# Low parts of weights by a negated copy and an accumulating transfer instead of a VectorE subtraction

## The chip, the cores and the metric

The kernel runs on one core of a Trainium2 chip. The metric is the device time of one execution in microseconds (us). The core has five engines with queues of their own, each worked through in order: TensorE (PE in the profile), VectorE (DVE), ScalarE (ACT), GpSimd (POOL) and SyncE (SP), which here issues the loads of weights. GpSimd and SyncE issue transfers (DMA) that 16 DMA engines carry out.

## The reference

One layer of a diffusion backbone over 128 context tokens and 512 latent tokens of width 1024, all in float32:

```python
def trunk_layer(x, cond, C0, n0, m0, rows, w_mod, ...):
    mod = jax.nn.silu(cond) @ w_mod + b_mod
    sh1, sc1, g1, shm, scm, gm, sh2, sc2, g2 = jnp.split(mod, N_MOD, axis=-1)
    h = modulate(rmsnorm(x, norm_g[0]), sh1, sc1)
    x = x + 0.5 * g1[:, None, :] * swiglu(h, ffn1_w1, ffn1_w2)
    h = modulate(rmsnorm(x, norm_g[1]), shm, scm)
    y, C, n, m = mixer(h, C0, n0, m0, rows, w_in, b_in, ...)
    x = x + gm[:, None, :] * y
    h = modulate(rmsnorm(x, norm_g[2]), sh2, sc2)
    x = x + 0.5 * g2[:, None, :] * swiglu(h, ffn2_w1, ffn2_w2)
    return x, C, n, m

def swiglu(h, w1, w2):
    a, b = jnp.split(h @ w1, 2, axis=-1)
    return (jax.nn.silu(a) * b) @ w2
```

The mixer projects h by w_in (9232 columns) to queries, keys, values, gates and the inputs of a short convolution, scans four heads in both directions in chunks of 128 tokens (mLSTM), and leads the results through w_ml_out, w_sc_out and w_o. At the end there is one more norm.

## The kernel before

**Products in three parts.** TensorE multiplies in a reduced form of float32 (float32r). So that nothing is lost, each operand is split in a high part, the rounded value, and a low part, the rest. A product is three matmuls of 128 x 128 weights against 320 tokens: high weights with high activations (line 238), high weights with low activations (239), low weights with high activations (240). The 640 tokens stand transposed, in two halves of 320.

**Splitting.** `split` makes both parts: ScalarE copies the raw values into a float32r tile (line 73), then VectorE subtracts that from the raw values (line 74). Weights use the tiles `wr` (raw, 128 x 1024, five buffers), `wh` and `wl` (high and low, 128 x 512, six buffers each). Activations use tiles named H..h and H..l, Uh and Ul, Bh and Bl, and go through the same function.

**Pairs.** Most of the projections (72 pairs of 128-column blocks) use Winograd's form of Strassen's algorithm: seven products in the place of eight, in the order A11, S1, S2, A12, S3, S4, A22. A11, A12 and A22 are blocks of the raw weights themselves, the "own blocks"; S1 to S4 are sums and differences of blocks that VectorE (for some pairs GpSimd) writes into `ws` tiles (line 211). Each product has 12 matmuls. Between the products ScalarE or VectorE copies partial sums out of PSUM or from one bank to another (lines 266, 272, 276, 284, 287, 290).

**Plain column blocks.** The second matrices of the feed-forwards (w2), w_ml_out, w_sc_out and most of w_o are multiplied block by block by `plain_el`: one raw tile, one or two operands of up to 512 columns, both token halves. `head_el` (the three pairs behind a norm) and `halves_el` (the last column blocks ahead of a norm) split their operands too. So do some units of the modulation, whose other units work from the raw tiles in float32 or on VectorE and are strewn between the elements.

**The order.** All is written out in one program, and each engine does its share in that order. `op()` hands out the next operand and first has the operands up to four places ahead cast (`cast_more`). A raw tile counts as done when its last reader has been emitted, and `load_more` then issues the next load on SyncE's queue, which waits until the buffer's readers are through:

```python
            split(o["ap"], hi[:, :w], lo[:, :w])
            optile[n] = (hi, lo)
            ptr["cast"] += 1
            rdone.update(o["last"])
            load_more()
```

**GpSimd** issues the transfers that hold no weights: x to and from memory between the mixer and the rest (`spill_x`, line 1058; line 1577), gates' rows and their products (1178, 1225, 1424), head results, the cached states (1248), new states (1330). It also adds a few tiles (lines 211, 752, 1229) and clears the two raw tiles of the gate columns (`gate_load`, line 1049), whose loads are the first of the mixer's head.

Of the kernel before, what the change touches and what calls it, by code (L numbers as in the profile page):

```python
# [44 lines left out]
def mixer_step(ctx: ExitStack, tc: tile.TileContext, x_prompt, x_sample, state_C, state_n, state_m,  # L45
# [26 lines left out]
    def split(raw, hi, lo):  # L72
        A.copy(hi, raw)  # L73
        V.tensor_sub(lo, raw, f32(hi))  # L74

    # ------------------------------------------------------------ program: weights run ahead of their use
    RAWB, OPB, SB, AHEAD = 5, 6, 4, 4
    raws, ops = [], []
    rtile, optile, rdone = {}, {}, set()
# [17 lines left out]
    def cast_more(upto):  # L97
        load_more()
        while ptr["cast"] < min(upto, ptr["held"] + OPB, ptr["cap"], len(ops)):
            n = ptr["cast"]  # L100
            if not ready(ops[n]):
                return
            while ptr["sum"] < min(n + 2, len(ops)) and ready(ops[ptr["sum"]]):
                o = ops[ptr["sum"]]
                o["ap"] = o["src"](o)
                ptr["sum"] += 1
            o = ops[n]
            w = o["n"]
            hi = ring.tile([P, 512], F32R, name="wh", bufs=OPB)
            lo = ring.tile([P, 512], F32R, name="wl", bufs=OPB)  # L110
            split(o["ap"], hi[:, :w], lo[:, :w])
            optile[n] = (hi, lo)
            ptr["cast"] += 1
            rdone.update(o["last"])
            load_more()
# [56 lines left out]
    def element(raws_, ops_, emit):  # L172
        return {"raws": raws_, "ops": ops_, "emit": emit}

    def step(fn):
        return element([], [], fn)
# [19 lines left out]
                              dap(w, row0 * ncol + col0, [[ncol, P], [P * ncol, nk], [1, P]]))  # L196
        return load

    # ------------------------------------------------------------ products
    # One pair of 128-column blocks of weights against both token halves: seven products (Winograd's form  # L200
    # of Strassen's algorithm over column blocks, halves of the contraction and halves of the tokens).
    LH, RH = slice(0, 512), slice(512, 1024)

    def pair_ops(r1=0, r2=1, e1=None):
        e1 = e1 or V

        def total(key, engine, fn, a, b):
            def src(o):
                g = o["group"].setdefault(r1, {})
                t = g[key] = ring.tile([P, 512], F32, name="ws", bufs=SB)  # L210
                getattr(engine, fn)(t, part(o, a), part(o, b))  # L211
                return t
            return src

        def part(o, key):
            if key[0] == "S":
                return o["group"][r1][key]
            return rtile[o["base"] + (r1 if key[1] == "1" else r2)][:, LH if key[2] == "1" else RH]

        whole = lambda key: lambda o: part(o, key)  # L220
        spec = lambda src, *r: {"raws": list(r), "n": 512, "src": src}
        return {
            "A11": spec(whole("A11"), r1), "A12": spec(whole("A12"), r1), "A22": spec(whole("A22"), r2),
            "S1": spec(total("S1", e1, "tensor_add", "A21", "A22"), r2),
            "S2": spec(total("S2", V, "tensor_sub", "S1", "A11"), r1, r2),
            "S3": spec(total("S3", e1, "tensor_sub", "A11", "A21"), r1, r2),
            "S4": spec(total("S4", V, "tensor_sub", "A12", "S2"), r1, r2),
        }
# [17 lines left out]
            late.pop(0)()  # L246

    def relax(left=1):
        """Emit what can wait no longer, with this many calls to come."""
        while lazy and len(lazy) >= left:  # L250
            lazy.pop(0)()

# [43 lines left out]
            yield  # L296

    def pair_el(load1, load2, ev, e1=None, units=(), spare_v=False):
        """units: elements with operands of their own, put between the products."""
        po = pair_ops(e1=e1)  # L300
        at_ = {1 + 2 * i: u for i, u in enumerate(units)}
        loads, ops_ = [load1, load2], []
        for i, name in enumerate(ORDER):
            ops_.append(po[name])
            if i in at_:
                ops_ += [dict(o, raws=[len(loads)], src=(lambda t, c: lambda o: rtile[o["base"] + t][:, c:c + 512])(
                    len(loads), c)) for c, o in zip((0, 512), at_[i]["ops"])]
                loads += at_[i]["raws"]

        def emit():  # L310
            nf = len(fill)
            for i, _ in enumerate(pair_steps(ORDER, ev, spare_v)):
                if i in at_:
                    at_[i]["emit"]()
                relax(7 - i)
                drain(nf - nf * (i + 1) // 7)
        return dict(element(loads, ops_, emit), pair=True)
# [20 lines left out]
        return HB["12" if k < 4 else "22"][k % 4]  # L338

    def head_el(p, chain, work, mid=()):  # L340
        """The three pairs behind a norm, without Strassen: three left halves first, row block by row block as the
        norm yields them, then what mid holds, while the right halves are made."""
        pre = len(mid) // 2
        order = [None] * pre + [0, 1, 2] + [None] * (len(mid) - pre) + [3, 4, 5]
        at_ = {t: i for i, t in enumerate(order) if t is not None}
# [56 lines left out]
        return el  # L402

    def halves_el(loads, nk, acts, ev, after):
        """Column blocks whose left halves all come first, then their right halves."""
        per = (nk + 3) // 4

        def emit():
# [34 lines left out]
    def plain_el(load, nk, acts, ev, halves=(0, 1)):  # L443
        def emit():
            nf = len(fill)
            ps = {h: big() for h in halves}
            w = [op() for _ in range(0, nk, 4)]
            n = 0
            for k in range(nk):
                hi, lo = w[k // 4]  # L450
                for h in halves:
                    three(ps[h][:, :HT], hi, lo, k % 4, acts(k, h), k == 0, k == nk - 1)
                relax(nk - k)
                drain(nf - nf * (k + 1) // nk)
            for h in halves:
                ev(h, ps[h][:, :HT])
            squares()
        return dict(element([load], tile_ops(nk), emit), calm=True)

    # ------------------------------------------------------------ constants  # L460
    zero = tp.tile([P, HT], mybir.dt.bfloat16, name="nrow")
    G.memset(zero, 0.0)
    ones = cst.tile([P, P], F32, name="ones")
# [39 lines left out]
            G.dma_start(gb[32 * d:32 * d + 4, i:i + 1], dap(b_in, off + 4 * d, [[1, 4], [1, 1]]))  # L503
        G.dma_start(m0[32 * d:32 * d + 4, :], dap(state_m, 4 * d, [[1, 4], [1, 1]]))

    # Sums seeded by a copy into PSUM go on accumulating: every bank they use has been written by the PE once.
    for i in range(4):
        PE.matmul(big()[:, :HT], zero[:, :P], zero, start=True, stop=True)

# [26 lines left out]
    def col(name, i):  # L536
        return vT[:, rows[name] + i:rows[name] + i + 1]

    # ------------------------------------------------------------ modulation
    PO = {}  # L540

    def mod_load(ch, half, kq):
# [4 lines left out]
        return load  # L547

    def mod_cols(ch, m0_, n, p, parts):
        """Rows of the modulation to columns, in three steps."""  # L550
        w = 2 * parts
        S = {}

# [59 lines left out]
    after = []  # L613

    def mod_mix(ch, half):
        """Half of a channel: units with split operands and units in float32 by turns."""
        S = {}

        def emit(w, kq):
# [67 lines left out]
        return units  # L687

    def with_units(main, units, spare=0):
        """Spread modulation units over elements; what a unit leaves to be done follows an element later."""  # L690
        out = []
        n, m = len(main) - spare, len(units)
        e = 0
# [31 lines left out]
            V.tensor_scalar(modT[:, ch], modT[:, ch], 0.5, None, op0=OP.mult)  # L725
        return f

    # ------------------------------------------------------------ norms
    X = [None] * KT
    sq, SQ = {}, []  # L730
    PIECES = ((0, 128, 192), (320, 448, 512))
# [82 lines left out]
        return f  # L814

    def right_chain(n, sh, first=False):
        """Steps in the order of head_el, and the sums of Strassen's algorithm that it makes by the way."""
        def all_of(*fs):
            def f():
                for x in fs:  # L820
# [57 lines left out]
        while SQ:  # L878
            SQ.pop(0)()

    # ------------------------------------------------------------ feed-forward
    GROUPS = (6, 6, 6, 4)

    def ffn(w1, w2, g, norm_, lists, units, e1=None, mid=()):
        """Elements: [head], then per group the other pairs and the column blocks of w2."""
        head, els, f0 = [], [], 0
        for size in GROUPS:
            U = {}
# [44 lines left out]
                        f()  # L933
        return after

    # ------------------------------------------------------------ start: x, first norm
    PO["u_x"] = ExitStack()

    def open_u():
# [77 lines left out]
                   mod_dve(SH2, (0,), ma_wide), 2)  # L1017
    prog += [step(gain(1, SCM)), step(lambda: PO["ma_x"].close()), w2s[-1]]

    # ------------------------------------------------------------ mixer  # L1020
    xd = dr.tile([KT, P, T], F32, name="xd")
    rd = dr.tile([KT, P, T], F32, name="rd")
    td = dr.tile([KT, P, T], F32, name="td")
# [214 lines left out]
    def head_steps(h):  # L1238
# [101 lines left out]
            return f  # L1340

        def rs_begin():
            """The mean squares to the power -0.5, by Newton's iteration from an estimate on the bits."""
            x = S["ss"]
            w = S["rs"] = PO["mlp"].tile([P, 2, NCH], F32, name="hrs")
            I32 = mybir.dt.int32
# [82 lines left out]
    def cx_pair(m):  # L1429
        def ev(mi, h, src):  # L1430
# [25 lines left out]
            for o, i in segs:  # L1456
                lazy.extend([side(o, i, True, False, w0), side(o, i, False, True, w2)])
        return z_load(C_OFF + m * P), z_load(X_OFF + m * P), ev

    h0 = head_q(0)  # L1460
    chain, work = right_chain(1, SHM)
    prog.append(head_el([(gate_load(IG_OFF), gate_load(FG_OFF), gate_ev), h0[0], h0[1]], chain, work,
                        mod_pe(GM, (0,), False)))
    prog += [step(spill_x), step(close_u), step(open_h1)]
    gate, NG = gates(), 38
    h1 = head_q(1)
    prog += weave([pair_el(*j, spare_v=True) for j in (h0[2], gml_pair(0), h1[0], h1[1])],
# [8 lines left out]
            jobs = [cx_pair(0), o_pair, cx_pair(1)]  # L1476
        prog += weave([pair_el(*j) for j in jobs], head_steps(h))

    # ------------------------------------------------------------ output side of the mixer
    def n_out():  # L1480
        p = aux()
        PE.transpose(p[:16, :P], nout, ident)
# [132 lines left out]
    prog.append(halves_el([w_load(w_o, 0, KT, m * P, D) for m in range(5, KT)], KT, y_acts,  # L1615
                          lambda m, h, ps: add_x(m + 5, h, ps, GM, True), after_lists(2, SH2)))

    # ------------------------------------------------------------ second feed-forward, output
    FN, YT = [], {}

    def fn_in():
# [89 lines left out]
```

## Time and profile before

| | |
|---|---|
| time, median of 3 runs | 1740.52 us (1740.15 to 1742.07) |
| profiled execution, span from the first to the last instruction | 1743.3 us; no other time is given for it |
| granted TensorE clock, mean | 0.995 |
| DMA | 193.13 MB, mean 111 GB/s |

The page gives each engine's busy time with its share of the span, and in the chain, followed back from the last instruction, whose work or wait filled the span. A group is a line of the kernel with its engine, operation, tiles and shape: count, busy us, mean ns of one, and the engine's idle time just before with what ended it. A wait reads "engine, tile and line that waited <- engine, tile and line that ended it: us in all, times, longest us". A timeline row gives start (us from the span's start), length (us), engine, line, operation and tiles. Matmuls follow each other closer than their lengths say, since they are pipelined.

### The profile page before, as it was taken

What the parts mean: (1) busy time and instruction counts of PE and PEld (TensorE: products, weight loads), DVE (VectorE), ACT (ScalarE), POOL (GpSimd) and SP (SyncE); (2) the same over time, 40 slices, a digit from 0 to 9 for tenths busy, and PEclk for the clock granted to TensorE, in tenths of its full rate; (3) what the DMA queues carried; (4) which work ended last, traced back from release to release, by engine and by line L of the source; (5) the groups of instructions that cost most, each with busy time, mean ns of one, the idle gap of its engine ahead of it and who ended that gap; (6) DMA issues with size and microseconds to landing.
All of it is one profiled execution on the core that took longest, in us unless ns stands there. A gap on an engine that the chain in (4) does not pass through costs nothing.

```text
span 1743.3 us, 29445 instructions
## 1 busy us (share of the span) xinstructions
PE 1706.1 (98%) x11169; PEld 1625.3 (93%) x11169; DVE 1299.9 (75%) x2742; ACT 814.4 (47%) x1749; POOL 169.5 (10%) x253
## 2 busy tenths in 40 slices
PE   8899999999999999999999999999999999999997
PEld 3889999999989899999999999999989999999997
DVE  5787787786868868787887788869767567467476
ACT  5553352452554675564653255542255435245253
POOL 1010000000030122111102222001100000000001
PEclk9899999999999999999999999999999999999999
DMA  8335334343343443333328433347432322322222
GB/s 290 100 116 150 86 112 119 97 116 115 95 111 112 99 115 82 88 101 78 105 87 270 145 85 86 99 142 217 136 94 62 101 73 68 103 73 85 82 77 61
DMA packets 273501, 193.13 MB, mean 111 GB/s; under 512 B 12179, under 2 KB 248346, under 8 KB 273360
## 3 DMA queue, kind: packets, MB, share of 16 engines
q1 hardware_dynamic: 264112, 161.96, 32.1%
q0 software_dynamic: 8480, 28.63, 5.9%
q8 instruction: 88, 1.44, 0.4%
q10 hardware_dynamic: 768, 0.66, 0.1%
q14 instruction: 53, 0.43, 0.1%
HBM read 175.92 MB, written 15.31 MB: 110 GB/s over the span
## 4 chain that ended last, share of the span: by engine, by line
PE 82%; DVE 8%; ACT 5%; issue 3%; DMA 2%; POOL 0%; ACTq 0%; DVEq 0%; POOLq 0%
PE ps L238 25%; PE ps L239 25%; PE ps L240 25%; DVE wl L74 2%; ACT wh L73 1%; PE ax L1292 1%; PE ax L1323 1%; PE ax L676 1%; DMA wr<-in_w_mod_dram 1%; PE ax L1295 1%; PE ax L582 1%; DVE ws L211 1%; DVE t L1436 1%; DVE x L1448 0%; PE ax L1269 0%
## 5 line engine op out<-in xcount | busy, mean ns | idle before, releaser
L74 DVE TENSOR_TENSOR wl<-wr,wh 128x512 fp32r<-128x512 f32 (+1 forms) x444 | 290.9, 671 | 96.2 <-ACT wh L73 94.3
L73 ACT CAST wh<-wr 128x512 fp32r<-128x512 f32 (+1 forms) x444 | 258.5, 595 | 195.8 <-PE ps L239 159.0
L74 DVE TENSOR_TENSOR wl<-ws,wh 128x512 fp32r<-128x512 f32 x288 | 202.8, 705 | 62.0 <-ACT wh L73 61.5
L73 ACT CAST wh<-ws 128x512 fp32r<-128x512 f32 x288 | 175.0, 618 | 105.7 <-DVE ws L211 63.9
L238 PE MATMUL ps<-Uh,wh 128*128 128x320 f32 x704 | 218.7, 311 | 0.0
L239 PE MATMUL ps<-Ul,wh 128*128 128x320 f32 x704 | 217.1, 308 | 0.0
L240 PE MATMUL ps<-Uh,wl 128*128 128x320 f32 x704 | 217.0, 308 | 0.0
L870 DVE SCALAR_TENSOR_TENSOR x<-ps,modT,x 128x128 f32<-128x128 f32 (+2 forms) x216 | 82.7, 433 | 121.8 <-PE ps L240 121.8
L238 PEld LDWEIGHTS ps<-Uh,wh 128*128 128x128 f32 x704 | 132.1, 188 | 2.6 <-issue 2.6
L238 PE MATMUL ps<-HT4h,wh 128*128 128x320 f32 x392 | 124.6, 318 | 8.2 <-ACT t L284 3.6
L239 PEld LDWEIGHTS ps<-Ul,wh 128*128 128x128 f32 x704 | 132.1, 188 | 0.2 <-DVE Ul L74 0.2
L240 PEld LDWEIGHTS ps<-Uh,wl 128*128 128x128 f32 x704 | 132.1, 188 | 0.0
L238 PE MATMUL ps<-H11h,wh 128*128 128x320 f32 x392 | 124.2, 317 | 1.7 <-ACT H11h L73 1.7
L239 PE MATMUL ps<-HT4l,wh 128*128 128x320 f32 x392 | 122.2, 312 | 0.7 <-DVE HT4l L74 0.7
L239 PE MATMUL ps<-H11l,wh 128*128 128x320 f32 x392 | 122.4, 312 | 0.1
L238 PE MATMUL ps<-H21h,wh 128*128 128x320 f32 x392 | 122.4, 312 | 0.0
L240 PE MATMUL ps<-H11h,wl 128*128 128x320 f32 x392 | 122.1, 311 | 0.0
L240 PE MATMUL ps<-HT4h,wl 128*128 128x320 f32 x392 | 122.1, 311 | 0.0
L240 PE MATMUL ps<-H21h,wl 128*128 128x320 f32 x392 | 121.3, 310 | 0.2 <-DVE wl L74 0.2
L239 PE MATMUL ps<-H21l,wh 128*128 128x320 f32 x392 | 121.1, 309 | 0.0
L238 PE MATMUL ps<-H22h,wh 128*128 128x320 f32 x360 | 113.0, 314 | 0.0
L240 PE MATMUL ps<-H22h,wl 128*128 128x320 f32 x360 | 111.7, 310 | 0.0
(380 smaller groups left out, 4560.0 us busy)
## 6 DMA issues: line engine op xcount, KB each, us to landing
wr<-in_ffn_w_dram SPq DMA_DIRECT2D x88, 512.0 KB, 3.9
wr<-in_w_mod_dram SPq DMA_DIRECT2D x72, 512.0 KB, 3.8
wr<-in_w_in_dram SPq DMA_DIRECT2D x72, 512.0 KB, 3.9
wr<-in_ffn_w_dram SPq DMA_DIRECT2D x48, 384.0 KB, 3.5
wr<-in_ffn_w_dram SPq DMA_DIRECT2D x16, 256.0 KB, 2.9
wr<-in_w_ml_out_dram SPq DMA_DIRECT2D x8, 512.0 KB, 5.0
wr<-in_w_sc_out_dram SPq DMA_DIRECT2D x8, 512.0 KB, 4.1
wr<-in_w_o_dram SPq DMA_DIRECT2D x8, 512.0 KB, 4.5
```

What stands on the lines that cost most here:

```text
L73: A.copy(hi, raw)
L74: V.tensor_sub(lo, raw, f32(hi))
L211: getattr(engine, fn)(t, part(o, a), part(o, b))
L238: PE.matmul(ps, hi[:, ws], ah, start=start, stop=False, skip_group_check=True)
L239: PE.matmul(ps, hi[:, ws], al, start=False, stop=False, skip_group_check=True)
L240: PE.matmul(ps, lo[:, ws], ah, start=False, stop=stop, skip_group_check=True)
L582: PE.matmul(hold["p"][:2, :], cm[:, 2 * kq + k, :], w[:, 512 * k:512 * k + 512], start=(kq == 0 and k == 0), stop=(kq == 3 and k == 1))
L676: PE.matmul(p[:2, j * n:j * n + n], sel[:, 2 * i:2 * i + 2], hold_[i][j], start=(i == 0), stop=(i == 1))
L870: V.scalar_tensor_tensor(X[m][:, o + a:o + b], ps[:, a:b], modT[:, g, m, cd:cd + 1], X[m][:, o + a:o + b], op0=OP.mult, op1=OP.add)
L1292: PE.matmul(p2[:, :DH + 1], S["q", dt][:, sl], S["C"][d][:, dt, :], start=(dt == 0), stop=(dt == 1))
L1295: PE.matmul(p1[:, :DH + 1], S["p", ch][:, d, :], PO["vt"][:, ch, :], start=True, stop=True)
L1323: PE.matmul(p[:, :DH + 1], kw[:, dt * P:(dt + 1) * P], PO["vt"][:, ch, :], start=True, stop=True)
```

## The change

A second way to split, `split_dma`, is added. ScalarE copies the raw values into the high part as before, then writes the negated high part into the low tile, and GpSimd issues a transfer that adds the raw values onto that tile in place. The operands marked `far` are split so: A11, A12 and A22 of every pair, and all operands of `plain_el`. Sums, activations, heads, `halves_el` and modulation units keep `split`. The stores of x (`spill_x`) are emitted ahead of the mixer's head instead of behind it. The other lines of the diff drop comments.

```diff
+    def split_dma(raw, hi, lo):
+
+        A.copy(hi, raw)
+        A.activation(lo, f32(hi), AF.Copy, scale=-1.0)
+        G.dma_start(f32(lo), raw, accum_op=OP.add)
...
-            split(o["ap"], hi[:, :w], lo[:, :w])
+            (split_dma if o.get("far") else split)(o["ap"], hi[:, :w], lo[:, :w])
...
-    def pair_ops(r1=0, r2=1, e1=None):
+    def pair_ops(r1=0, r2=1, e1=None, far=True):
...
-            "A11": spec(whole("A11"), r1), "A12": spec(whole("A12"), r1), "A22": spec(whole("A22"), r2),
+            "A11": dict(spec(whole("A11"), r1), far=far), "A12": dict(spec(whole("A12"), r1), far=far),
+            "A22": dict(spec(whole("A22"), r2), far=far),
...
-        return dict(element([load], tile_ops(nk), emit), calm=True)
+        return dict(element([load], [dict(o, far=True) for o in tile_ops(nk)], emit), calm=True)
...
     h0 = head_q(0)
     chain, work = right_chain(1, SHM)
+    prog.append(step(spill_x))
     prog.append(head_el([(gate_load(IG_OFF), gate_load(FG_OFF), gate_ev), h0[0], h0[1]], chain, work,
                         mod_pe(GM, (0,), False)))
-    prog += [step(spill_x), step(close_u), step(open_h1)]
+    prog += [step(close_u), step(open_h1)]
```

## The prediction

> **What bounds the kernel.** I read the page's sums and chain first, then the waits of TensorE, then stretches of the span, and last single pairs in the timeline.
>
> ```profile
> span 1743.3 us, 29445 instructions
> PE 1706.1 (98%) x11169; PEld 1625.3 (93%) x11169; DVE 1299.9 (75%) x2742; ACT 814.4 (47%) x1749; POOL 169.5 (10%) x253
> PE 82%; DVE 8%; ACT 5%; issue 3%; DMA 2%; POOL 0%; ACTq 0%; DVEq 0%; POOLq 0%
> ...
> 0.00:50.00 50.00, 39.05 (x148) 15.93 (x149) 30.53 (x99) 27.20 (x67) 8.57 (x27) 0.99 0.85 276
> 1700.00:1750.00 50.00, 33.64 (x236) 32.12 (x234) 28.28 (x99) 15.14 (x33) 8.71 (x10) 0.93 0.18 53
> ```
>
> TensorE is idle for 37 us (1743.3 less 1706.1). The first 50 us hold 11 of these, and the 43 us of the span in the last window hold 9.7. Both lie outside the changed operations. So 16 or 17 us at most can be won in between, whatever VectorE is spared.
>
> ```profile
> PE ps L238 <- ACT t L284: 3.6, 2, 1.8
> PE ps L238 <- DVE t L287: 2.6, 3, 1.1
> PE ps L238 <- ACT ps L266: 2.5, 4, 1.1
> PE ps L238 <- ACT ps L276: 1.7, 5, 0.4
> PE ps L240 <- DVE wl L74: 0.2, 1, 0.2
> ```
>
> These are TensorE's waits inside the pairs. The low parts (wl, line 74) stop it for 0.2 us in the whole span. What stops it are copies out of PSUM: 7.8 us by ScalarE and 2.6 us by VectorE. VectorE is 75% busy, but its subtractions run ahead of their use.
>
> **The change, part by part.** The kernel makes 72 pairs with three own blocks each (216) and 142 operands of plain column blocks: 358 low parts change, 310 of 512 columns and 48 of 256.
>
> ```profile
> L74 DVE TENSOR_TENSOR wl<-wr,wh 128x512 fp32r<-128x512 f32 x396 | 273.8, 702 | 91.2 <-ACT wh L73 89.3
> L74 DVE TENSOR_TENSOR wl<-wr,wh 128x256 fp32r<-128x256 f32 x48 | 20.1, 418 | 5.0 <-ACT wh L73 5.0
> L73 ACT CAST wh<-wr 128x512 fp32r<-128x512 f32 x396 | 240.1, 618 | 161.6 <-PE ps L239 124.7 <-DMA wr<-in_w_ml_out_dram 23.4 <-DMA wr<-in_w_mod_dram 9.5
> L73 ACT CAST wh<-wr 128x256 fp32r<-128x256 f32 x48 | 19.4, 404 | 34.3 <-PE ps L239 34.3
> L751 ACT ACTIVATE t<-x 128x320 f32<-128x320 f32 x42 | 19.6, 471 | 72.2 <-DVE x L870 61.8 <-issue 10.3
> ```
>
> *VectorE.* Removed: 310 x 0.702 + 48 x 0.418 = 238 us of busy time. It pays only where TensorE waits for VectorE, or for a ScalarE held up by VectorE. The first is the 2.6 us of line 287; the ScalarE copies could add 7.8. Bounds 0 and -10; I take -3, because the ScalarE copies get more in front of them (next).
>
> *ScalarE.* Added: one negation each. The trace has none of this form; a cast of that size takes 0.618 us and an ACTIVATE of 320 columns 0.471, so I take 0.62 (0.40 for 256 columns): 310 x 0.62 + 48 x 0.40 = 211 us. Where ScalarE has room this costs nothing:
>
> ```profile
> 1430.00:1504.00 74.00, 74.00 (x507) 74.00 (x506) 51.25 (x97) 36.27 (x78) 0.00 (x0) 1.00 0.30 88
> 1007.00:1113.00 106.00, 104.54 (x708) 103.49 (x707) 92.70 (x160) 59.53 (x121) 18.51 (x14) 1.00 0.32 84
> 1056.28 0.62 ACT L73 CAST wh<-wr 128x512 fp32r<-128x512 f32 x1
> 1056.81 0.42 ACT L276 COPY ps<-ps 128x320 f32<-128x320 f32 x1
> 1057.28 0.41 PE L238 MATMUL ps<-HT3h,wh 128*128 128x320 f32 x1 [0.32 <-ACT ps L276]
> ```
>
> The columns of a window are its length, then busy us (instructions) of PE, PEld, DVE, ACT and POOL, the clock, the DMA share and GB/s. In the second feed-forward (first row) TensorE never rests and ScalarE is idle half the time. In the convolution pairs (second row, 1007 to 1113) the own block A22 is cast just ahead of the copy of line 276 that TensorE then waits for. The negation goes between the two, so such a wait grows by up to 0.62. There are five of line 276 and six of lines 266 and 284: 0 to +6.8 us if each grew in full. Some will be shortened by the spared VectorE; I take +3.
>
> *The low part's path.* Before: cast, then 0.70 us on VectorE. Now: cast, negation 0.62, POOL starts, the transfer lands. POOL's start is taken from a store that waits for ScalarE (637.67 + 0.56 to 638.53: 0.30 us). The transfer itself is in no trace. Its nearest rows are transfers of 256 KB:
>
> ```profile
> 637.67 0.56 ACT L1423 ACTIVATE t<-t,biT 128x320 f32<-128x320 f32 x1
> 638.53 0.58 POOL L1424 DMA_DIRECT2D gd<-t  x1 [3.73 <-ACT t L1423]
> L1330 POOL DMA_DIRECT2D out_dram<-Cc x8: 715/722/732, 648.3 to 860.4; - x8
> DMA to landing us min/median/max: 2.5/2.6/4.3
> L1248 POOL DMA_DIRECT2D C<-in_state_C_dram x8: 722/722/732, 623.8 to 831.1; - x8
> DMA to landing us min/median/max: 3.0/3.2/5.1
> q0 software_dynamic: 8480, 28.63, 5.9%
> xd<-x POOLq DMA_DIRECT2D x8, 320.0 KB, 7.0
> ```
>
> A store of that size lands after 2.6 us. By POOL's queue (q0: packets, MB, share of the 16 engines) 28.63 MB cost 5.9% of the span, 3.6 us per MB, so 0.94 us for 0.262 MB. The addition also reads what it adds to, at worst another 0.94. I take 3.3, between 2.6 and 3.5; the ends are 2.5 (quickest store) and 7.0 (eight 320 KB stores at once). From the end of the cast a low part is then there after 0.62 + 0.30 + 3.3 = 4.2 us. The Trainium skill's page "DMA: Bandwidth & Descriptors", section "Anatomy of one DMA — SWDGE (gpsimd) path", fits about 2 us plus bytes over 436 GB/s, an estimate of 2.6 us here; the store of this trace agrees. Its page "Collectives: The Full Stack" (on the bandwidth ceiling) says that an add in the DMA path is held back by its two source reads, and this speaks against the change: with the data time doubled the fit estimates 3.2 us. With 3.2 for my 3.3 the sum would be about 0.5 us lower, with 2.6 about 3 us lower; no run here shows the doubling.
>
> Against 4.2 us stands the time from the cast's end to the first matmul on the low part:
>
> ```profile
> 1477.14 0.61 ACT L73 CAST wh<-wr 128x512 fp32r<-128x512 f32 x1
> 1483.02 0.31 PE L240 MATMUL ps<-H21h,wl 128*128 128x320 f32 x1
> 1061.19 0.31 PE L240 MATMUL ps<-HT4h,wl 128*128 128x320 f32 x1
> 688.14 0.60 ACT L73 CAST wh<-wr 128x512 fp32r<-128x512 f32 x1
> 692.02 0.31 PE L240 MATMUL ps<-H21h,wl 128*128 128x320 f32 x1
> 117.90 0.61 ACT L73 CAST wh<-wr 128x512 fp32r<-128x512 f32 x1
> 120.60 0.31 PE L240 MATMUL ps<-H21h,wl 128*128 128x320 f32 x1
> ```
>
> In a steady pair (first two rows) A12 is the tightest: 1483.02 - 1477.75 = 5.27 us, so a transfer may take 4.35. The convolution's A22 (cast at 1056.28) has 4.29 us and just holds. A12 behind a head's end (688, three times) has 3.28: short by 0.9. A12 among the modulation's units in the first pairs (117, three times) has 2.1 in the row shown: short by 2.1. Six more are short by 0 to 0.5. Together 8 us in 12 operands. Stalls of neighbours cover each other, and VectorE is spared just there: I take +5 (bounds 0, and the third rival). Plain blocks cast two operands ahead and are not short.
>
> *POOL's queue.* 358 issues of 0.54 to 0.72 us, some 230 us on an engine at 10%, are hidden as work. But what waits on POOL now stops low parts:
>
> ```profile
> 612.14 0.56 POOL L1178 DMA_DIRECT2D decB<-decd  x1 [6.45 <-DMA decd<-sm_de]
> ```
>
> For these 6.45 us the queue is shut while A22, A11 and A12 of the next pairs come up: 0 to +6, taken +2.5. The waits of line 1248 and of the gates' memsets look longer only because POOL arrives early. The eight stores of spill_x move ahead of the head and of the gate loads' memsets; POOL issues them in about 4.4 us and nothing stands behind them yet: 0 (1 either way).
>
> *Raw tiles and transfers.* A raw tile is freed when the transfer has landed, about 3.5 us later than by subtraction. In pairs its buffer is needed again only five raw tiles, two and a half pairs, later: 0. The transfers move 310 x 0.262 + 48 x 0.131 = 87.5 MB, 18% of the span at the plain price, 36% at twice. The tight places:
>
> ```profile
> 920.00:978.00 58.00, 56.26 (x375) 54.04 (x374) 41.23 (x73) 15.86 (x32) 11.47 (x20) 1.00 0.78 245
> 1166.00:1262.00 96.00, 95.44 (x638) 90.62 (x636) 83.15 (x192) 25.51 (x52) 14.68 (x24) 1.00 0.61 183
> ```
>
> In the first, 16 transfers add 4.2 MB x 3.6 = 15 us of 58, taking 0.78 to 1.04; in the second, 26 add 24.5 of 96, 0.61 to 0.87. Bounds 0 and +17; with a depth of five raw tiles I take +1.5.
>
> Sum: -3 + 3 + 5 + 2.5 + 1.5 = +9 us. The profiled execution spans 1743.3 us, 2.8 above the runs' median of 1740.5; the page gives nothing around the span. On the span this is 1752.3, on the median **1749.5**.
>
> **The rivals.** *Faster:* the spared VectorE brings ScalarE's casts and copies forward in the mixer, the transfers land in the store's 2.6 us or so, and none is late. All waits of lines 284, 287, 266 and 276 (10.4 us) are the most; at a little over half, 1734.5. It decides if the transfer lands within about 3 us. For it: those waits hang on a backlog that VectorE shares. Against: the copies stand behind the new negations.
>
> *Nothing to see:* the terms cancel, 1740.5. For it: TensorE is at 98%, and the steady pairs hide 4.35 us. A difference under 0.2%, 3.5 us, cannot be told from no change here.
>
> *Late in every pair:* the transfer lands after more than 4.35 us, because the addition is slow or meets a weight load, and then each of 72 pairs waits at A12 for what is over. At 5.0 this is 72 x 0.65 = 47 us, with the other terms about 1796; at 5.5, some 1832. For it: the largest rows are 4.3 to 7.0. Against: their medians of 256 KB are 2.6 and 3.2.
>
> **How the numbers follow.** My forecast, slower by 4 to 25 us at a few short leads, has 0.42; late in every pair 0.16; nothing to see 0.22; faster 0.20. So faster 0.20, same 0.22, slower 0.58. The range 1733 to 1790 leaves out a third of the faster case and most of the third rival, under 2 in 10; the forecast's own range is 1744 to 1766.
>
> **What would show it.** Right: VectorE's busy time down by about 238 us and ScalarE's up by 211; transfers landing at 3 to 4 us; new waits of line 240's matmuls on a DMA at about 104 to 140, 600 to 615 and 690 to 840, none after 1300; the waits on line 276 longer. Wrong: landing above 4.4 with a wait in each pair, or TensorE's waits on lines 284 to 287 gone with no new ones.

## The result and the profile after

The changed kernel takes 1814.04 us (median of 4 runs, 1811.16 to 1816.48), 1.0418 times the kernel before (95% interval 1.0401 to 1.0434). The forecast was 1749.5, with a range up to 1790. The sign was right; the size was not: +74 us where +9 stood. One execution in the experiments, the profiled one of e8, ran at a granted clock of 0.557 (2786.71 us) and is not counted. The change adds six lines ahead of most of the code and a seventh behind them, so line 211 is now 217, 238 is 245, 239 is 246, 240 is 247, 266 is 273, 276 is 283, 284 is 291, 287 is 294; the new cast, negation and transfer are lines 78, 79 and 80.

The page after: span, engines, chain, GpSimd's transfer queue (packets, MB, share of 16 engines), then the new groups, the landing of the 256 KB transfers at the median of the page, and of all of them at least, median and most.

```profile
span 1814.7 us, 30387 instructions
PE 1729.9 (95%) x11169; PEld 1636.5 (90%) x11169; DVE 1106.9 (61%) x2384; ACT 1023.4 (56%) x2107; POOL 480.1 (26%) x611
q0 software_dynamic: 60032, 116.21, 35.1%
PE 61%; issue 13%; DMA 11%; DVE 6%; ACT 5%; POOL 3%; POOLq 0%; ACTq 0%; SPq 0%; DVEq 0%
L80 POOL DMA_DIRECT2D wl<-wr x358 | 314.5, 887 | 1099.7 <-ACT wl L79 681.8
L79 ACT ACTIVATE wl<-wh 128x512 fp32r<-128x512 f32 (+1 forms) x358 | 216.0, 603 | 11.4
wl<-wr POOLq DMA_DIRECT2D x310, 256.0 KB, 3.9
DMA to landing us min/median/max: 3.2/4.0/9.2
```

VectorE has 193 us less to do and ScalarE 209 more. TensorE was idle for 37 us and now is for 85; besides, the same 11169 matmuls keep it busy for 1729.9 us in place of 1706.1. So 48 of the 71 us between the two spans are new idle time and 24 are longer matmul time. What ended TensorE's idle time in the pairs and plain blocks (us in all, times, longest):

```profile
PE ps L247 <- DMA wl<-wr: 21.9, 25, 3.4
PE ps L245 <- DVE t L294: 15.5, 11, 2.9
PE ps L245 <- DVE x L1532: 7.1, 2, 4.4
PE ps L245 <- ACT ps L273: 6.6, 6, 2.8
PE ps L245 <- ACT t L291: 2.4, 3, 1.0
PE ps L245 <- ACT ps L283: 1.5, 4, 0.9
```

Where the loss lies follows from the first matmul on the first operand of each stage, the same in every kernel. The table gives the stage's length before and what each profiled execution adds to it, in us. The start (to the first pair) differs by -5.5 to +1.8 whatever is changed, and isn't argued from.

| kernel | start | first 3 pairs | rest of first feed-forward | 18 pairs woven with the gates and heads | two gml pairs | w_ml_out | first bg pair behind it | other bg and cx pairs | gsc, sc, w_o, head | second feed-forward | end |
|---|---|---|---|---|---|---|---|---|---|---|---|
| before, length | 98.4 | 47.5 | 419.1 | 331.8 | 29.6 | 58.9 | 14.8 | 113.4 | 175.6 | 415.9 | 38.3 |
| after | -2.4 | +8.8 | +4.5 | +20.7 | +0.5 | +11.1 | +6.3 | +17.2 | +2.1 | +0.8 | +1.9 |
| e1, sums on VectorE | +0.1 | +6.5 | +3.7 | +25.5 | +0.4 | +7.2 | 0.0 | -1.3 | +1.5 | +1.1 | +0.8 |
| e2, before, sums on VectorE | -5.4 | -2.1 | -0.1 | +0.5 | -1.2 | 0.0 | 0.0 | -2.3 | 0.0 | 0.0 | +0.1 |
| e3, VectorE adds | +1.5 | +0.2 | 0.0 | +14.0 | +2.5 | +0.3 | 0.0 | +10.4 | +6.5 | 0.0 | +0.1 |
| e4, plain blocks alone | -3.2 | 0.0 | +0.1 | +0.4 | +0.3 | +3.1 | +4.6 | +0.1 | +1.7 | 0.0 | +0.1 |
| e5, plain copy | -2.5 | +5.5 | +1.6 | +12.2 | -0.2 | +0.9 | +0.5 | +8.2 | 0.0 | 0.0 | +0.7 |
| e6, copy from ScalarE | -2.1 | +2.6 | +2.9 | +27.2 | +3.6 | +1.9 | +6.3 | +15.8 | +0.4 | +1.9 | +0.2 |
| e7, heads' pairs as before | -4.4 | +8.7 | +4.0 | +0.3 | +0.3 | +3.4 | +2.3 | +13.4 | +4.2 | +2.7 | +0.9 |
| e10, VectorE negates | -1.6 | +8.9 | +8.1 | +14.7 | +1.6 | +10.3 | +5.8 | +16.9 | +7.9 | +5.9 | +1.0 |
| e11, three places mended | -2.2 | +6.1 | +4.3 | +0.1 | +0.5 | 0.0 | 0.0 | -1.6 | +1.8 | +2.3 | +0.4 |
| e12, no transfers, sums on VectorE | -5.5 | -2.1 | -0.1 | +0.6 | -1.4 | 0.0 | 0.0 | -2.3 | 0.0 | 0.0 | +0.1 |
| e13, ScalarE's load alone | +1.8 | 0.0 | +0.1 | +8.0 | +0.3 | 0.0 | 0.0 | +3.4 | 0.0 | 0.0 | +0.1 |
| e14, heads' pairs alone | -1.9 | 0.0 | 0.0 | +21.9 | -0.5 | 0.0 | 0.0 | +0.1 | 0.0 | 0.0 | +1.1 |

The second feed-forward, with the largest number of steady pairs, loses 0.8 us. The loss sits in four places: the first three pairs, the heads' pairs, w_ml_out with the pair behind it, and the convolution's pairs.

**Why a wait costs more than itself.** Three waits of TensorE show it, the first and the last on a transfer. Timeline rows of TensorE (for the first also of ScalarE and GpSimd), then windows behind the wait (length, busy us of PE, PEld, DVE, ACT and POOL, clock, DMA share, GB/s):

```profile
107.59 0.63 ACT L79 ACTIVATE wl<-wh 128x512 fp32r<-128x512 f32 x1
108.52 0.87 POOL L80 DMA_DIRECT2D wl<-wr  x1 [6.76 <-ACT wl L79]
112.87 0.42 PE L247 MATMUL ps<-HT4h,wl 128*128 128x320 f32 x1 [2.03 <-DMA wl<-wr]
114.00:117.00 3.00, 3.00 (x13) 3.00 (x12) 2.10 (x5) 0.40 (x1) 0.00 (x0) 0.50 0.71 219
118.00:121.00 3.00, 3.00 (x20) 2.46 (x19) 0.34 (x1) 2.82 (x6) 1.16 (x2) 1.00 0.10 29
1028.02 0.39 PE L245 MATMUL ps<-H11h,wh 128*128 128x320 f32 x1 [4.40 <-DVE x L1532]
1029.00:1038.00 9.00, 6.26 (x24) 5.89 (x24) 6.91 (x10) 2.24 (x5) 2.85 (x4) 0.50 0.88 246
1039.00:1045.00 6.00, 6.00 (x33) 4.25 (x32) 2.11 (x5) 2.21 (x5) 4.38 (x4) 1.00 0.57 83
964.45 0.42 PE L247 MATMUL ps<-Bh,wl 128*128 128x320 f32 x1 [2.19 <-DMA wl<-wr]
965.00:969.00 4.00, 4.00 (x30) 4.00 (x29) 0.50 (x1) 2.39 (x4) 0.90 (x2) 1.00 1.02 323
```

After 2.03 us without a matmul TensorE is granted half its clock for about 3.4 us: 13 matmuls in 3 us, then 20. After the waits of 4.40 and 2.74 us near 1028 half clock lasts for 10 us. Over the whole span TensorE is busy at half clock for 40.8 us, and for 13.0 us in the kernel before. Half of the difference, some 14 us, is what half clock adds, an estimate; the other 10 of the 24 us of longer matmul time were not followed up. A wait of 2 us with 3.4 us at half clock behind it costs about 2 + 1.7 = 3.7. Behind the first 50 us TensorE stops ten times for 1.96 us or more while at full clock: nine times half clock follows, once (2.19 us at 964.45) it doesn't. It follows none of the stops of up to 1.6 us.

### The profile page after: what moved, and what is told of

Its sections match the earlier page's. It is cut to its first block, busy times and chain, and to the rows that moved or that the text cites. A ratio compares the mean times of both kernels' runs of the same rounds, so it can differ in the third digit from the quotient of the medians.

```text
span 1814.7 us, 30387 instructions
## 1 busy us (share of the span) xinstructions
PE 1729.9 (95%) x11169; PEld 1636.5 (90%) x11169; DVE 1106.9 (61%) x2384; ACT 1023.4 (56%) x2107; POOL 480.1 (26%) x611
## 3 DMA queue, kind: packets, MB, share of 16 engines
q0 software_dynamic: 60032, 116.21, 35.1%
## 4 chain that ended last, share of the span: by engine, by line
PE 61%; issue 13%; DMA 11%; DVE 6%; ACT 5%; POOL 3%; POOLq 0%; ACTq 0%; SPq 0%; DVEq 0%
PE ps L247 19%; PE ps L245 19%; PE ps L246 18%; DMA wl<-wr 6%; DMA wr<-in_w_sc_out_dram 1%; POOL wl L80 1%; DVE wl L74 1%; PE ax L1330 1%; PE ax L1299 1%; POOL ws L217 1%; PE ax L683 1%; ACT wh L73 1%; ACT wh L78 1%; PE ax L1302 1%; PE ax L589 1%
## 5 line engine op out<-in xcount | busy, mean ns | idle before, releaser
L80 POOL DMA_DIRECT2D wl<-wr x358 | 314.5, 887 | 1099.7 <-ACT wl L79 681.8
L78 ACT CAST wh<-wr 128x512 fp32r<-128x512 f32 (+1 forms) x358 | 210.3, 587 | 181.0 <-PE ps L246 71.8
L79 ACT ACTIVATE wl<-wh 128x512 fp32r<-128x512 f32 (+1 forms) x358 | 216.0, 603 | 11.4
```

Of the source, the lines that this page charges most:

```text
L79: A.activation(lo, f32(hi), AF.Copy, scale=-1.0)
L80: G.dma_start(f32(lo), raw, accum_op=OP.add)
```

## The experiments

**e1. Sums on VectorE.** GpSimd made S1 and S3 of 13 pairs, ten in the convolution (cx and bg) and the first three (26 sums in the trace; the expectation counts 16 pairs), and these sums stood in its queue among the transfers.

```diff
-            prog += [pair_el(*cx_pair(m), G), pair_el(*cx_pair(m + 1), G)]
+            prog += [pair_el(*cx_pair(m)), pair_el(*cx_pair(m + 1))]
...
```

`G` goes in the same way for the bg pairs and the first three pairs.

> The changed kernel, but VectorE makes the sums S1 and S3 of the 13 convolution pairs and the first three pairs of the first feed-forward, which GpSimd made. Theory 'sums in POOL's queue': these sums stand behind accumulating transfers that wait for ScalarE, so they come late, and with them S2, S4 and the copies out of PSUM. Then the stretch from the first bg pair to the first gsc pair, 152 us after the change (1028 to 1180) against 128 before, falls by 15 to 25 us, and the whole from 1814 to 1790 to 1800. Rival 'late low parts': the transfers themselves come too late; then the stretch stays within 5 us of 152. Rival 'ScalarE is full': also unchanged, or longer, since nothing is taken off ScalarE.

Measured: 1792.69 us, 1.0285 (1.0254 to 1.0316). As the theory had it, the bg and cx pairs' +17.2 became -1.3; the first pairs' +8.8 became +6.5. The changed kernel's rows in one cx pair (GpSimd, VectorE, ScalarE, TensorE) show why:

```profile
1099.14 0.85 POOL L80 DMA_DIRECT2D wl<-wr  x1 [4.00 <-ACT wl L79]
1099.70 1.62 POOL L217 TENSOR_TENSOR ws<-wr 128x512 f32<-128x512 f32 x1
1101.57 1.91 POOL L217 TENSOR_TENSOR ws<-wr 128x512 f32<-128x512 f32 x1
1101.35 2.68 DVE L217 TENSOR_TENSOR ws<-ws,wr 128x512 f32<-128x512 f32 x1 [2.55 <-POOL ws L217]
1104.07 0.62 ACT L73 CAST wh<-ws 128x512 fp32r<-128x512 f32 x1 [2.10 <-DVE ws L217]
1105.10 0.41 PE L245 MATMUL ps<-HT4h,wh 128*128 128x320 f32 x1 [1.58 <-DVE t L294]
```

The transfer at the head of GpSimd's queue waits 4.00 us for its negation. The sum behind it needs no negation, yet starts only then; VectorE's sum waits 2.55 us for it, ScalarE's cast for VectorE, and TensorE for a VectorE whose copy out of PSUM is behind all that.

**e2. The same on the kernel before**, as a control.

> The kernel before with the same edit (VectorE makes the sums of those 16 pairs): the control for the run beside it. VectorE was busy for 92.7 of 106 us in the convolution pairs, and 32 sums of 0.68 us are added, 26 of them there: I expect 0 to +12 us against before. If this control is faster than before by as much as the other run is faster than the change, the sums on GpSimd were bad anyway and the transfers are not their cause.

Measured: 1738.46 us, 0.9979 (0.9969 to 0.9988). It is a little faster where I had expected 0 to 12 us slower: on GpSimd the sums cost the kernel before 2.1 us in the first pairs and 2.3 in the convolution. So of the 18.5 us that e1 wins in the convolution some 16 are the queue's.

**e3. Negation kept, VectorE adds.**

```diff
-        G.dma_start(f32(lo), raw, accum_op=OP.add)
+        V.tensor_add(lo, raw, f32(lo))
```

> The changed kernel with VectorE adding the raw weights onto the negated copy in place of the transfer: ScalarE's 358 negations stay, VectorE has its 238 us back, no transfer is made. Rival 'ScalarE is full': most of the 74 us stays, 1790 or more. Theories 'sums in POOL's queue', 'late low parts' and 'full DMA engines': it falls near to before, 1740 to 1755, the rest being what the negations cost.

Measured: 1778.4 us, 1.0214 (1.0199 to 1.0229), between the two ranges that were expected. Without any transfer 37 us are lost, 14.0 and 10.4 of them in the heads' and the convolution's pairs. TensorE waits for copies of ScalarE:

```profile
PE ps L245 <- ACT ps L283: 9.0, 8, 2.1
PE ps L245 <- ACT ps L273: 7.3, 8, 2.0
PE ps L245 <- ACT t L291: 4.1, 3, 1.8
```

This looked like ScalarE's load alone; by e13 a third of it is.

**e4. Plain blocks alone**: `far` only in `plain_el`.

> The changed kernel with far only in plain column blocks (142 low parts); the 216 own blocks of pairs are subtracted on VectorE again. Theory 'full DMA engines' for the ml stage: its 8 blocks stay at about 70 us against 59 before, the bg pair behind them stays late by some 6, and the whole is 1750 to 1762. If the ml stage recovers to 59 here, it was hurt by a backlog that the pairs ahead of it bring along, not by its own transfers, and the whole is 1740 to 1745. All three theories say that the pairs' stages go back to their times before.

Measured: 1753.7 us, 1.0077 (1.0059 to 1.0095). The time is within the expectation, the stage isn't: w_ml_out with the pair behind it loses 3.1 + 4.6 = 7.7 us in place of 17.4, though all its own transfers stay. The rest goes with the pairs' transfers.

**e5. A plain copy in place of the addition.** The kernel leaves out the addition, so its low parts are the raw weights.

```diff
-        G.dma_start(f32(lo), raw, accum_op=OP.add)
+        G.dma_start(f32(lo), raw)
```

> The changed kernel, but the transfer copies the raw weights onto the low tile and adds nothing (so the low parts are the raw weights). Theory (four places: GpSimd's sums behind waiting transfers, 21 us; ScalarE in the mixer's pairs, 14; late transfers there and in the first pairs, 15; the DMA engines in w_ml_out and behind it, 17): only what hangs on the landing and on the DMA engines gets smaller, so the issue falls from 0.86 us to about 0.6, the landing from 4.0 to about 3, and the time from 1814 to 1797 to 1806; the convolution's pairs keep their loss. Rival A (the adding transfer's price is the cause): most of the 74 us goes, below 1775. Rival B (ScalarE's work is the cause): 1810 to 1816.

Measured: 1775.44 us, 1.0186 (1.015 to 1.0222): 39 us less than with the addition, just above the bound that rival A had. The queue, GpSimd's issues, and the landings of this run:

```profile
q0 software_dynamic: 35584, 116.21, 19.5%
L80 POOL DMA_DIRECT2D wl<-wr x358 | 193.4, 540 | 1168.1 <-ACT wl L79 753.7
wl<-wr POOLq DMA_DIRECT2D x310, 256.0 KB, 2.6
```

For the same bytes an adding transfer takes 35.1% of 1814.7 less the 103 us that the queue had before, 534 us of the 16 engines; a plain one 242. That is 2.2 times, 6.1 against 2.8 us per MB. Its issue takes 0.887 us in place of 0.540 and it lands 1.3 us later. So my expectation (8 to 17 us) was too small: the price of the addition hits all four places, the convolution's pairs too (17.2 to 8.2), whose loss I had expected to stay. The Trainium skill says ("Collectives: The Full Stack", section "The bandwidth ceiling: the fold count and why AG ≠ RS ≠ AR") of the adding step of a collective that it is held to half the rate of a copy by its two source reads; the factor of 2.2 here is near to that, and no run here shows the reads.

The stage of w_ml_out, first before, then after, then with the plain copy:

```profile
926.40:985.30 58.90, 58.90 (x395) 56.95 (x394) 43.67 (x74) 13.34 (x25) 12.25 (x20) 1.00 0.72 225
958.50:1028.40 69.90, 60.53 (x394) 57.03 (x394) 28.78 (x51) 21.58 (x39) 24.17 (x33) 1.00 0.97 249
943.00:1002.80 59.80, 59.44 (x395) 56.96 (x394) 32.31 (x54) 22.25 (x40) 20.78 (x36) 1.00 0.94 305
```

With additions the DMA engines are 97% busy for 70 us at 249 GB/s; with copies they carry 305 and the stage is done in 60. The weights of the stage wait for the same engines: ScalarE's casts for them 32.2 us, where the row of before has 23.4 (window 955 to 1050 of the changed kernel):

```profile
ACT wh L78 <- DMA wr<-in_w_ml_out_dram: 32.2, 6, 7.2
DVE x L1532 <- DMA x<-gd: 19.5, 5, 6.9
wl<-wr POOLq DMA_DIRECT2D x20, 256.0 KB, 6.0
```

**e6. The copy issued by ScalarE.** As e5, with `A.dma_start(f32(lo), raw)`.

> As the run with the plain copy, but issued from ScalarE's queue just behind the negation, so GpSimd's queue holds none of the 358 transfers and its sums are free. Theory: the loss of the convolution's pairs (about 20 us) goes, and the wake of GpSimd (0.3 us) with it, so 18 to 25 us below the run with the plain copy, about 1780, if an issue costs ScalarE little; at 0.1 us more per issue in the mixer some 5 us of that come back. Rival B (ScalarE's work is the cause): not below the run with the plain copy, rather above it. Rival A (transfer's price): the same as the run with the plain copy.

Measured: 1805.15 us, 1.0342 (1.0312 to 1.0373), 30 us above e5 where 18 to 25 below were expected. An issue holds ScalarE for 0.47 us, 358 x 0.472 = 169 us that the page doesn't count as busy; the row of the next cast shows ScalarE idle for 0.55 us, the issue included.

```profile
L80 ACTq DMA_DIRECT2D wl<-wr x358: 472/472/545, 81.6 to 1754.6; - x179
1056.69 0.47 ACTq L80 DMA_DIRECT2D wl<-wr  x1
1057.20 0.46 ACT L73 CAST Bh<-x 128x320 fp32r<-128x320 f32 x1 [0.55 <-ACT wl L79]
```

The first three pairs fell to +2.6, the heads' pairs rose to +27.2. The convolution's pairs still lose 15.8, though GpSimd's sums are free there: TensorE now waits for ScalarE's copies of line 283 (11.1 us of its waits between 1035 and 1180). Here a free queue of GpSimd only moved the wait to ScalarE.

**e7. The 20 pairs woven with the heads as before** (`far=False` there).

> The changed kernel, with the subtraction by VectorE again in the 20 pairs that are woven with the gates and the heads' steps (60 low parts). Theory: the 21 us lost there go, nothing else changes: 1790 to 1796. Rival (the pairs are late because VectorE or ScalarE carry a backlog from elsewhere): under 8 us, 1806 to 1814. Rival A (transfer's price alone, with ScalarE free): the same 1790 to 1796, but then the run with ScalarE's negation and VectorE's addition should have lost nothing there, and it lost 14.

Measured: 1781.31 us, 1.0212 (1.0185 to 1.024), 9 us better than expected. The heads' +20.7 became +0.3, and w_ml_out with its pair fell from 17.4 to 5.7, though nothing was changed there: in the two gml pairs just ahead the DMA share falls from 0.88 to 0.64.

**e8. w_ml_out's blocks as before.**

> The changed kernel, with the subtraction by VectorE again in the column blocks of w_ml_out alone (16 low parts of 512 columns). Theory (the DMA engines are full there, raw tiles wait for landings of 6 to 9 us and the weight loads behind them): the 11 us of that stage go and 3 to 6 us of the pairs behind it, 1797 to 1803. Rival (the stage is late because x and the state come back late, on whatever path): 1 to 3 us, 1811 to 1813. Rival B (ScalarE): at most 16 x 0.6 = 10 us of work less, 1806 to 1812, with the DMA waits of the weight loads as long as before.

Measured: 1796.69 us (median of the three that count), 1.0297 (1.0254 to 1.034), at the lower edge of the expectation. There are no rows for it.

**e9. More work for ScalarE, in fp8**: behind VectorE's subtraction, a negated copy to an fp8 scratch tile.

> VectorE subtracts as in the kernel before and no transfer is issued; behind the subtraction's issue ScalarE writes a negated copy of up to 440 columns of each of the 358 high parts onto a small scratch tile that nobody reads, about 190 us of work more on ScalarE and no low part later. Theory (ScalarE's time is the cause of 14 of the 21 us in the mixer's pairs and of 10 in the convolution's): 1758 to 1770, with TensorE waiting longer for ScalarE's copies out of PSUM. Rival (not ScalarE's time but the low part that comes later through the negation): 1740 to 1747.

Measured: 1865.47 us, 1.0703 (1.0688 to 1.0718). Not the load that was meant: 93 table loads stand at the line of the saturating fp8 write, and other lines of ScalarE have more of them than before.

```profile
L80 ACT ACTIVATE more<-wh 128x440 fp8e4<-128x440 f32 (+1 forms) x358 | 197.1, 551 | 9.5
L80 ACT ACT_TABLE_LOAD x93 | 119.3, 1283 | 1.6
```

ScalarE got 407 us more. The run decides nothing here; e13 repeats it without the table loads.

**e10. VectorE negates, the transfer adds.**

```diff
-        A.activation(lo, f32(hi), AF.Copy, scale=-1.0)
+        V.tensor_scalar(lo, f32(hi), -1.0, None, op0=OP.mult)
```

> The changed kernel, but VectorE writes the negated high part instead of ScalarE, so ScalarE is as loaded as before the change, VectorE too, and the transfers with GpSimd's queue stay. Theory: the part of ScalarE goes, 10 to 20 us, 1794 to 1804; the late landings, GpSimd's sums and the w_ml_out stage stay. Rival A (the adding transfer alone): 1810 to 1818.

Measured: 1826.14 us, 1.0487 (1.0467 to 1.0508), slower than the change, though ScalarE is as loaded as before it (814.6 us) and a negation takes 0.43 us there. The heads' pairs won 6 us, but both feed-forwards and the sc and w_o stages lost 14 more: the negation now waits in VectorE's queue, and in the second feed-forward TensorE's waits for low parts rise from 0.2 to 4.5 us.

```profile
PE ps L247 <- DMA wl<-wr: 36.9, 32, 4.2
L79 DVE TENSOR_SCALAR wl<-wh 128x512 fp32r<-128x512 f32 (+1 forms) x358 | 150.7, 430 | 143.7 <-ACT wh L78 140.8
```

So my theory (10 to 20 us won) missed, but the run doesn't isolate ScalarE's share. In the heads' pairs TensorE's waits for copies of lines 273 and 294 fall from 10.7 to 3.5 us, and those for low parts rise from 5.6 to 12.7: later transfers take back part of what an unburdened ScalarE gives.

**e11. Three places mended**: e1, e7 and e8 in one kernel; 282 transfers stay.

> The changed kernel with three places mended together: VectorE subtracts again in the 20 pairs woven with the heads and in w_ml_out, and VectorE makes the sums S1 and S3 that GpSimd made; 282 of the 358 transfers stay. Theory (the places are told apart, 33 and 15 and 21 us, with some counted twice): 1745 to 1753, with 7 to 9 us left in the first three pairs of the first feed-forward and no stage else over 3. Rival (every transfer costs, 0.2 us each): 282 x 0.2 = 56 us, about 1797.

Measured: 1756.42 us, 1.0073 (1.0056 to 1.0089), 3 us above the expectation and 41 below the rival. The kernel to set it against is e12, which has these sums on VectorE and no transfer: 1738.46 us. So 282 transfers cost 18 us, 8.2 of them in the first three pairs and 4.4 in the rest of that feed-forward (over the 3 that I had allowed). That is 0.06 us for a transfer. The change, with the 76 others and GpSimd's sums, takes 58 us more than e11: the place counts.

**e12. No low part by transfer, sums on VectorE, stores of x early.**

> The kernel before with VectorE making S1 and S3 of the convolution's and first pairs, and the eight stores of x emitted ahead of the mixer's head; no low part by transfer. The sums alone gave 0.9979 of the time before. Theory (the stores' place is worth nothing): the same, 0.997 to 0.999, 1736 to 1740. Rival (stores ahead of the head's loads hold them up): 1742 to 1748.

Measured: 1738.46 us, 0.9969 (0.9958 to 0.9981): the same as e2. The stores' place is worth nothing that can be told, and the fastest versions measured have none of the new transfers.

**e13. ScalarE's load alone.** Subtraction by VectorE, and two negated pieces that nobody reads:

```diff
+        V.tensor_sub(lo, raw, f32(hi))
+        for i in range(2):
+            A.activation(more, f32(hi)[:, 64 * i:64 * i + 64], AF.Copy, scale=-1.0)
```

> VectorE subtracts as in the kernel before and no transfer is issued; behind each of the 358 subtractions ScalarE writes two negated pieces of 64 columns onto a scratch tile that nobody reads, about 0.59 us or 211 us in all, as much as the negations of the change. Theory (ScalarE's time costs the heads' pairs by itself): 8 to 14 us there, 1750 to 1760 in all. Rival (it is the low part that comes later, through negation, queue and transfer): 0 to 4 us there, 1740 to 1746.

Measured: 1754.55 us, 1.007 (1.0051 to 1.0089). The heads' pairs lose 8.0, the convolution's 3.4, no other stage behind the start over 0.3:

```profile
L81 ACT ACTIVATE more<-wh 128x64 f32<-128x64 f32 x716 | 184.2, 257 | 22.7
PE ps L247 <- ACT ps L275: 5.5, 7, 1.2
PE ps L247 <- ACT ps L285: 5.4, 6, 1.1
```

(Lines 247, 275 and 285 of that kernel are the changed kernel's 245, 273 and 283.) With 184 of the change's 216 us, ScalarE's occupation costs 12 us. The other 25 of e3 are left, by subtraction, for a low part that VectorE can only make behind the negation, and for the 32 us less of work; no run parts these.

**e14. The change in the 20 pairs woven with the heads alone.**

> The change in the 20 pairs woven with the gates' and heads' steps alone (60 low parts), all else as before. Theory (these pairs lose by themselves): their 21 us, 1759 to 1764. Rival (a backlog from elsewhere, GpSimd's queue or the DMA engines, makes most of it): under 8 us, 1741 to 1748.

Measured: 1765.68 us, 1.0129 (1.011 to 1.0147), 2 us above the expectation. They lose 21.9 by themselves and nothing changes elsewhere, so no backlog from other stages is needed. The worst wait in them, on the transfer of an A22, with GpSimd's rows ahead of it and TensorE's clock behind it:

```profile
600.07 2.89 POOL L1232 DMA_DIRECT2D wt<-nmd  x4 [0.72 <-DMA nmd<-row_e]
602.95 1.86 POOL L80 DMA_DIRECT2D wl<-wr  x2
609.35 0.63 PE L247 MATMUL ps<-HT4h,wl 128*128 128x320 f32 x1 [4.12 <-DMA wl<-wr]
611.09 0.57 POOL L1185 DMA_DIRECT2D decB<-decd  x1 [5.73 <-DMA decd<-sm_de]
610.00:613.00 3.00, 3.00 (x13) 3.00 (x13) 0.69 (x1) 0.00 (x0) 1.47 (x2) 0.50 0.76 179
```

The A22's transfer stands behind four gate transfers of 2.89 us in GpSimd's queue and lands at 609.30; TensorE stops for 4.12 us and goes on at half clock. decB's wait of 5.73 us comes only behind that transfer.

## Why the prediction was right or wrong

The way of the change was forecast, but not what it costs: four terms of the sum were too small, most of all GpSimd's queue (2.5 for some 16 us) and raw tiles and transfers (1.5 for 17.4 us), and the clock had none.

**The path of a low part: right in its parts, short in the landing.** Negation 0.62, start 0.30 and landing 3.3 were forecast; the trace has 0.603, 0.29 to 0.30 (the transfer at 108.52 behind the negation that ended at 108.22) where GpSimd is free, and landings of 3.2 at the least, 3.9 at the median and 9.2 at the most. The lead of the steady pairs was long enough even so, and with that the largest rival falls: "late in every pair" gave 1796 to 1832, which fits the time, but the second feed-forward's pairs lost under 1 us. A time that fits a rival doesn't make the rival true. After 1300 TensorE waits 0.2 us in all for a transfer of a low part, as forecast.

**Low parts that are short, +5: mis-sized.** The shortfalls listed for it already make 3 x 0.9 + 3 x 2.1 = 9.0 us without the six others, where the prediction says 8. In the first three pairs, which lose 8.8 us, I had named A12. Its three waits are 1.17, 0.50 and 0.53 us, and the plain copy of e5 removes them. The two longest, 2.03 and 2.00 us, are on A22, and half clock follows both. A22's transfers start 0.30 us behind their negations (row at 108.52) and stand behind no sum, but land after 4.3 and 4.7 us. These two waits stay with the sums on VectorE (1.94 and 1.90 us in e1) and with the plain copy (2.38 and 2.61 in e5), so neither the sums nor the price of the addition is their cause. Without transfers the three pairs lose 0.2 us (e3). Late landings are shown; what delays these two stays open. Of the 21.9 us that TensorE waits for low parts, some 12 lie in the first and the heads' pairs, where I looked for them, and some 9 in the rest of the first feed-forward, the gml pairs and w_ml_out, where I had none.

**GpSimd's queue, +2.5: the step that failed first.** I put transfers behind GpSimd's other work and asked what is late; I never put GpSimd's other work behind the transfers, though the sums that GpSimd makes were named in the description. A transfer that waits for a negation shuts the queue: some 16 us in the convolution's pairs (e1 less e2). The other stop that this term named, at 600 to 615, came in the right place by another cause: TensorE's longest wait for a low part, 3.40 us, ends at 621.33 on a transfer behind the four gate transfers, as in the rows of e14. decB's wait begins behind that transfer, and TensorE doesn't stop for the one behind decB.

**ScalarE, +3: mis-sized.** Alone it is 12 us (e13), 8.0 in the heads' pairs and 3.4 in the convolution. In the changed kernel the waits for line 276 (now 283) are 1.5 us after 1.7, though I had said that they would grow; those for line 266 (now 273) grew from 2.5 to 6.6. My bound of 6.8 let only the eleven existing waits grow. In e13, of the 13 waits shown, nine stand at matmuls that waited before, and seven of these grew by 0.47 to 0.78 us, near the 0.62 that I had; four are new, 0.54 to 0.76 us each. And ScalarE's copies hold on less in the heads than the mean of 47% says: the stretch 565 to 897 had 199.27 busy us in 331.8, 60%.

```profile
565.00:896.80 331.80, 324.80 (x2076) 309.54 (x2076) 260.80 (x623) 199.27 (x450) 59.74 (x99) 0.99 0.36 91
```

**Raw tiles and transfers, +1.5: mis-sized, at its own upper bound.** The DMA share in w_ml_out was forecast at 1.04 and the bound at +17. The share became 0.97 and the loss 11.1 + 6.3 = 17.4, and 1.4 with plain copies; with VectorE's subtraction in this stage alone the kernel is 17 us faster (e8). I had worked out that the engines are full and then let five raw tiles hide it. They couldn't: the raw tiles' own loads pass through the same full engines, and so do the gate rows that come back from memory into x tiles (x<-gd): VectorE's product with them (line 1532) is late, and TensorE stops 4.40 us and 2.74 us for it.

**VectorE, -3:** its busy time fell by 193 us, not 238 (line 74's alone by 226; the sums took 13 more than before, and the rest was not broken down). No run isolates what this won; no stage became shorter.

**What had no term: the clock.** Some 14 of the 71 us are matmuls at half clock behind waits of about 2 us or more. Each term was priced as the wait alone. The Trainium skill has this ("TensorE: Matmul & The Clock Gate", sections "Part 1: The HAM clock gate (the "warmup" mystery)" and "HAM oscillation — how this bites in real kernels"), with idle time of about 3.4 us as the limit; in this trace waits of 1.96 to 2.07 us sufficed, so here the measurement decides. Its half rate and its time of some 3.4 us until full rate agree with the rows. It also says that the window of 3.4 us runs on its own; that could be why one wait of 2.19 us was not followed by half clock, which no run here shows.

The steps overlap, so the parts found singly don't add up to 74: the addition's own price is 39 (e5), the queue with sums 21 less the 3.5 that e2 wins (e1), the heads' pairs as a whole 33 with what they do to w_ml_out (e7). What stays open: the 10 us (12.6 against e12) that e11 leaves in the first feed-forward, of which only the first pairs' waits were looked into, and how the heads' 21 divide, where ScalarE's 8.0 alone and the addition's 8.5 (20.7 less e5's 12.2) would leave 4 for queue and copy if they added up, which no run shows.

## What to carry to other kernels

In this kernel, work moved to a transfer was cheap only where its lead was long, its queue held nothing that others wait for, and the DMA engines had room: look at these three by stage, and put the transfer only there. When a queue gets new waiting entries, list what stands behind them as well as what stands ahead. Price a TensorE wait of about 2 us or more at its length and 1.7 us, for the half clock that followed nine of ten of them here.

## What the runs showed of the hardware

- An adding transfer between SBUF tiles of 256 KB took GpSimd 0.887 us to issue against 0.540 for a plain one, landed in 3.9 against 2.6 us (medians) and used 2.2 times the DMA time per byte.
- The same plain transfer issued from ScalarE held ScalarE's queue for 0.47 us (e6).
- Behind the first 50 us, after nine of ten stops of TensorE of 1.96 us or more at full clock, the granted clock was 0.5 for about 3.4 us (10 us behind the stops near 1028); after stops of up to 1.6 us it stayed at 1.
- A VectorE sum of two SBUF tiles took 2.68 us where GpSimd's sum ran beside it; the median of 72 is 0.69:

```profile
L217 DVE TENSOR_TENSOR ws<-ws,wr x72: 669/691/2685, 90.4 to 1747.4; 128x512 f32<-128x512 f32 x72
```

- The line of e9's 358 saturating writes to fp8 on ScalarE has 93 table loads of 1.283 us; the float32 writes of e13 have none. Which of the two, the type or the saturation, brings them is not shown.
